# Splitting the weights of the layers' first halves in the DMA queue of a DeltaNet, S5 and pooling backbone

## The chip, the cores and the metric

The kernel runs on one core of a Trainium2 chip. The metric is the time of one execution on the device in microseconds; the time before is the median of three runs. The engines are named as in the profile: PE is TensorE's matmuls and PEld its weight loads, DVE is VectorE, ACT is ScalarE, POOL is GpSimd, and SP is the engine that only issues DMAs here. POOL can issue DMAs as well, on a queue of its own.

## What is computed

Two streams go through two layers with shared weights: 128 context tokens and 512 latent tokens, 1024 channels each, float32. The reference, cut to what matters:

```python
def trunk_layer(x, cond, s_dn, s_re, s_im, ...):
    mod = (silu(cond) @ w_ada + b_ada)[:, None, :]
    shift1, scale1, gate1, shift2, scale2, gate2 = split(mod, 6)
    h = rmsnorm(x, norm1_g) * (1 + scale1) + shift1
    q, k, v, z, dn_a, dn_b, u_ssm, u_pool, gates = split(h @ w_in, offsets)
    o_dn = deltanet_mixer(q, k, v, z, dn_a, dn_b, ...)   # 4 heads x 128, chunks, both directions
    o_ssm = s5_mixer(u_ssm, ...)                         # 32 groups, 64 complex states, both directions, GLU
    o_pool = pool_mixer(u_pool, ...)                     # centred windows 2, 4, 8, 16
    g_dn, g_ssm, g_pool = split(sigmoid(gates), 3)
    merged = g_dn * (o_dn @ w_branch_dn) + g_ssm * (o_ssm @ w_branch_ssm) + g_pool * (o_pool @ w_branch_pool)
    x = x + gate1 * (merged @ w_out)
    h = rmsnorm(x, norm2_g) * (1 + scale2) + shift2
    return x + gate2 * conv_ffn(h, ffn_w_up, ffn_conv, ffn_w_down)
```

A layer's first half is everything up to `x + gate1 * ...`, its second half is the ConvFFN.

## The kernel before

Activations lie with the channels on the partitions and all 640 tokens side by side, in two halves of 320 columns. A large product is made tile by tile: 128 output channels over 4 or 8 blocks of 128 input channels. This text calls one such tile with its weights a **piece**: a piece of 8 blocks has 512 KB of weights, a piece of 4 blocks 256 KB.

Products are made with float32r operands in three parts. Every operand is split into a high part, its cast to float32r, and a low part, the rest. `mm3` (L377) multiplies high by high, high by low and low by high (L384, L386, L388), so there are six matmuls of 320 columns per block, 48 in a piece of 8 blocks.

The weights come raw. `wraw` (L356) loads a piece on SP's queue into one of `WRAW` = 4 buffers. `wsplit` (L362) then splits it in steps of `WK` = 4 blocks: ScalarE casts 128x512 values into a `whi` tile, through a helper whose line in the profile is L235, and VectorE subtracts (L372):

```python
S.activation(hi, src, AF.Copy)
V.tensor_sub(lo, src, hi)
```

There are `WB` = 4 buffers of half a piece for each part. The tag `wraw` also holds the conditioning weights (`wada`, multiplied at L446).

In a first half two kinds of work run side by side. A **chain** is a long dependent computation: first the S5 scan, later DeltaNet. The S5 chain begins with products of its parameters on VectorE and POOL (L900, L901, L906). DeltaNet uses VectorE throughout (for example L1457, L1467) and POOL for scalings (L1534, L1535). **Side work** is a queue of pieces in `Weave` (L189), each with a cost, a function and, as a third entry, a function that fetches its weights. `Weave.run` pulls pieces as the chain yields costs, and `step` (L209) fetches the weights of the next piece just before it makes the current one. The pieces of a layer, in order: z gates and pooling inputs (`zgate`, `pool`, 4 each), the pooling branch's gates and projections in turn (`gated`, 8 pairs of 8 and 4 blocks), 8 of the q, k, v inputs (`qkv`), all beside the S5 scan; then the four GLU pieces (`glu`) and 8 pairs for the S5 branch, with no chain beside them, which this text calls the stage of the S5 gates; then 4 more of q, k, v and 8 gates beside DeltaNet. The projections of the DeltaNet branch, the output projection and the FFN take their weights through `Stream.tile` in plain loops.

The function texts set only the program's order; a scheduler then orders each engine's instructions. Each engine runs its own list strictly in that order, and a DMA waits in the list of the engine that issues it.

## Time and profile before

| | |
|---|---|
| median of three runs | 2593.4 us (2589.87 to 2594.01) |
| the profiled execution | 2591.93 us |
| its span in the profile | 2590.2 us, 43654 instructions |
| mean granted clock of TensorE | 0.973 |
| HBM read, written | 251.45 MB, 42.48 MB |

The profile shows one execution. Its span runs from the first instruction to the end of the last; the 1.7 us beside it are the rest of the execution's own time. Stages can be told from DMAs: in layer 0 the first GLU weight is asked for at 317.5 us (the end of the S5 chain), DeltaNet's first decay row at 534.9, the first weight of the output projection at 768.8, the first of the FFN at 810.9; in layer 1 the first half lies between about 1345 and 2070 us. Matmuls are pipelined: two of the same line that stand together in the timeline overlap, and the pace is the distance between starts, not the length of one.

### The profile page before, as it was taken

The numbers are of one execution on the slowest core, as the hardware profiler recorded it, in microseconds if no ns is written. First come the engines' busy times: TensorE is split into PE (matmuls) and PEld (weight loads), VectorE is DVE, ScalarE is ACT, GpSimd is POOL, SyncE is SP. The second block draws the span as 40 slices with busy tenths as digits, with TensorE's granted clock in tenths as the row PEclk, the third lists the DMA queues.
The fourth block names the chain that finished last, engine by engine and source line by source line (L and its number), as shares of the span: only waits on it lengthen the run. The fifth ranks groups of instructions, "written<-read, shape, count | busy, mean of one in ns | idle before, by whom it ended". The sixth has DMA issues, their size and how long they took to land. (4 is left out here: it accounts for less than half of the span.)

```text
span 2590.2 us, 43654 instructions
## 1 busy us (share of the span) xinstructions
PE 2440.7 (94%) x17225; PEld 2321.6 (90%) x17225; DVE 1608.3 (62%) x3250; ACT 989.8 (38%) x1792; POOL 555.2 (21%) x560
## 2 busy tenths in 40 slices
PE   7899989998889999999988999899989999999999
PEld 6688987997789988999988998799879899999998
DVE  5768863269866743553596687633897766445355
ACT  4242342363333531442443423424533354334243
POOL 3521320135342100000134404311445320000000
PEclk8899999999889999999999999999999999999999
DMA  9833327344253255322237232463454322222221
GB/s 309 162 112 94 91 64 233 114 127 140 94 178 95 74 172 178 98 67 81 75 115 103 59 113 79 118 197 99 138 166 160 112 66 74 74 74 78 78 66 66
DMA packets 382016, 297.29 MB, mean 115 GB/s; under 512 B 33706, under 2 KB 336500, under 8 KB 381812
## 3 DMA queue, kind: packets, MB, share of 16 engines
q1 hardware_dynamic: 377892, 286.53, 38.4%
q0 software_dynamic: 3552, 7.73, 1.2%
q8 instruction: 136, 2.23, 0.4%
q14 instruction: 68, 0.56, 0.1%
q10 hardware_dynamic: 368, 0.25, 0.0%
HBM read 251.45 MB, written 42.48 MB: 113 GB/s over the span
## 5 line engine op out<-in xcount | busy, mean ns | idle before, releaser
L384 PE MATMUL acc<-pg,whi 128*128 128x320 f32 x4064 | 943.2, 313 | 5.9 <-ACT pg L235 2.9
L388 PE MATMUL acc<-pg,wlo 128*128 128x320 f32 x4064 | 936.0, 311 | 8.0 <-DVE wlo L372 8.0
L386 PE MATMUL acc<-pg,whi 128*128 128x320 f32 x4064 | 938.0, 311 | 4.9 <-DVE pg L411 4.9
L372 DVE TENSOR_TENSOR wlo<-wraw,whi 128x512 fp32r<-128x512 f32 (+1 forms) x538 | 414.5, 776 | 524.3 <-ACT whi L235 518.1
L384 PEld LDWEIGHTS acc<-pg,whi 128*128 128x128 f32 x4064 | 681.4, 189 | 47.1 <-issue 16.7
L388 PEld LDWEIGHTS acc<-pg,wlo 128*128 128x128 f32 x4064 | 684.5, 189 | 10.5 <-DVE wlo L372 8.9
L386 PEld LDWEIGHTS acc<-pg,whi 128*128 128x128 f32 x4064 | 685.4, 189 | 6.0 <-DVE pg L411 5.4
L235 ACT ACTIVATE whi<-wraw 128x512 fp32r<-128x512 f32 (+1 forms) x538 | 331.7, 623 | 925.4 <-PE acc L386 723.0
L235 ACT ACTIVATE pg<-pg 128x640 f32<-128x640 f32 (+8 forms) x335 | 222.0, 682 | 262.5 <-DVE pg L1996 56.1
L235 ACT ACTIVATE pg<-sm 128x512 f32<-128x512 f32 (+9 forms) x245 | 109.5, 470 | 207.1 <-PE sm L1502 59.4
L235 ACT ACTIVATE pg<-acc 128x640 f32<-128x640 f32 (+3 forms) x196 | 127.0, 655 | 73.9 <-PE acc L388 49.5
L700 DVE SCALAR_TENSOR_TENSOR pg<-pg,cols_f 128x511 f32<-128x511 f32 (+1 forms) x130 | 65.9, 548 | 49.8 <-ACT pg L235 49.7
L411 DVE TENSOR_TENSOR pg<-pg,pg 128x640 fp32r<-128x640 f32 x84 | 68.6, 821 | 41.4 <-ACT pg L235 37.6
L713 POOL DMA_DIRECT2D pg<-in_ssm_lambda_re_dram x2 | 1.2, 583 | 407.9 <-ACT whi L235 407.9
L1685 POOL TENSOR_TENSOR pg<-pg,pg 128x640 f32<-128x640 f32 x21 | 38.9, 1855 | 226.1 <-DVE pg L1683 146.9
L691 DVE SCALAR_TENSOR_TENSOR pg<-acc,mod,pg 128x320 f32<-128x320 f32 x56 | 30.8, 549 | 78.3 <-PE acc L388 78.2
L235 ACT ACTIVATE pg<-acc,cols_f 128x640 f32<-128x640 f32 (+1 forms) x88 | 68.3, 776 | 0.0
L701 DVE SCALAR_TENSOR_TENSOR pg<-pg,cols_h 128x511 f32<-128x511 f32 (+1 forms) x130 | 65.6, 546 | 0.0
L446 PE MATMUL sm<-wada,silu_c 128*32 128x512 f32 x320 | 57.9, 627 | 8.0 <-DMA wada<-in_w_ada_dram 8.0
L1683 DVE SCALAR_TENSOR_TENSOR pg<-pg,acc 128x640 f32<-128x640 f32 x48 | 39.0, 817 | 40.9 <-PE acc L388 35.3
L906 POOL TENSOR_TENSOR pg<-pg,pg 128x512 f32<-128x512 f32 (+1 forms) x32 | 54.7, 1710 | 1.9
L901 POOL TENSOR_TENSOR pg<-s_cp,pg 128x640 f32<-128x640 f32 x16 | 27.6, 1725 | 127.4 <-PE acc L388 55.8
(392 smaller groups left out, 2960.8 us busy)
## 6 DMA issues: line engine op xcount, KB each, us to landing
wraw<-in_w_in_dram SPq DMA_DIRECT2D x96, 512.0 KB, 4.4
wraw<-in_ffn_w_up_dram SPq DMA_DIRECT2D x88, 512.0 KB, 3.9
wada<-in_w_ada_dram SPq DMA_DIRECT2D x80, 512.0 KB, 4.4
wraw<-in_ffn_w_down_dram SPq DMA_DIRECT2D x32, 512.0 KB, 3.9
mg_dram<-pg SPq DMA_DIRECT2D x32, 320.0 KB, 2.2
pg<-mg_dram SPq DMA_DIRECT2D x32, 320.0 KB, 5.2
wraw<-in_w_out_dram SPq DMA_DIRECT2D x16, 512.0 KB, 3.9
pg<-in_w_ada_dram SPq DMA_DIRECT2D x6, 1024.0 KB, 10.8
```

What stands on the lines that cost most here:

```text
L235: ins = self.engine.activation(out, in_, func, **kw)
L372: V.tensor_sub(lo, src, hi)
L384: PE.matmul(ps[:M, h, :HF], hi[:, k, :M], hh[:, h * HF:(h + 1) * HF], start=first and k == 0, stop=False)
L386: PE.matmul(ps[:M, h, :HF], hi[:, k, :M], hl[:, h * HF:(h + 1) * HF], start=False, stop=False)
L388: PE.matmul(ps[:M, h, :HF], lo[:, k, :M], hh[:, h * HF:(h + 1) * HF], start=False, stop=last and k == n - 1)
L411: V.tensor_sub(lo.r, src, hi.r)
L446: PE.matmul(ps[q:q + 32, :], silu_c[:, k, :], t[:, j * 512:(j + 1) * 512], start=k == 0, stop=k == KT - 1, tile_position=(0, q))
L700: V.scalar_tensor_tensor(y[:, b + 1:e], r[:, b:e - 1], w0, y[:, b + 1:e], op0=OP.mult, op1=OP.add)
L701: V.scalar_tensor_tensor(y[:, b:e - 1], r[:, b + 1:e], w2, y[:, b:e - 1], op0=OP.mult, op1=OP.add)
L906: E.tensor_tensor(oo, oo, t.f, op=OP.add if r else OP.subtract)
L1683: V.scalar_tensor_tensor(hv(g_.f), hv(g_.f), 1.0, ps[:, :, :HF], op0=OP.add, op1=OP.mult)
L1685: GP.tensor_tensor(g_.f, g_.f, mg.f, op=OP.add)
```

## The change

For 64 pieces of each layer (those with `dma=True`: all gates, z, pooling, q, k, v, GLU, and the projections of the pooling and S5 branches) the split is made another way. `wdma` has POOL issue a DMA that casts the weights to float32r while loading them into `whi`. ScalarE writes the negated high part into `wlo`, in one pass over the piece. POOL then issues a second DMA of the same weights that adds them onto `wlo`. VectorE and SP have no part in it. 44 of these pieces have 8 blocks, 20 have 4. `Weave` now fetches the weights of the next two pieces.

The constants change for all weights: a part of a piece is one tile of up to 8 blocks (`WK` = 8) with three buffers (`WB` = 3), so that `wsplit`, which stays for the other weights, makes one pass in place of two; there are three raw buffers; one page of the buffer arena is 128 columns smaller.

```diff
--- before.py
+++ after.py
@@ -35,10 +35,10 @@
 NSLOT = 82
 UNIT = 4
 PAGE = 2592 // UNIT
-PAGES = [5888] + [2592] * 2 + [2560] * 4 + [1280] * 11 + [2592]
+PAGES = [5760] + [2592] * 2 + [2560] * 4 + [1280] * 11 + [2592]
 EPS = 1e-6
-WRAW = 4
-WK, WB = 4, 4
+WRAW = 3
+WK, WB = 8, 3
 OFF_Q, OFF_K, OFF_V, OFF_Z, OFF_AB = 0, 512, 1024, 1536, 2048
 OFF_SSM, OFF_POOL, OFF_G = 2064, 2576, 3088
 POOL_WINDOWS = (2, 4, 8, 16)
@@ -194,7 +194,7 @@
         self.arena = arena
         self.q = deque()
         self.credit, self.scale = 0.0, 1.0
-        self.w = None
+        self.w = deque()
 
     def add(self, cost, fn, weights=None):
 
@@ -209,8 +209,12 @@
     def step(self):
         cost, fn, weights = self.q.popleft()
         self.arena.side = True
-        w = [self.w or weights()] if weights else []
-        self.w = self.q[0][2]() if self.q and self.q[0][2] else None
+        if weights and not self.w:
+            self.w.append(weights())
+        w = [self.w.popleft()] if weights else []
+        later = [x for _, _, x in self.q if x][:2]
+        while len(self.w) < len(later):
+            self.w.append(later[len(self.w)]())
         fn(*w)
         self.arena.side = False
         self.credit -= cost
@@ -374,6 +378,17 @@
             los.append(lo)
         return Blocks(his), Blocks(los)
 
+    def wdma(src, c0, nk):
+
+
+        v = src.rearrange("(k p) m -> p k m", p=P)[:, :, c0:c0 + P]
+        hi = wpool.tile([P, nk, P], F32R, name="whi", tag="whi", bufs=WB, padded_shape=[P, WK, P])
+        lo = wpool.tile([P, nk, P], F32R, name="wlo", tag="wlo", bufs=WB, padded_shape=[P, WK, P])
+        GP.dma_start(hi, v)
+        S.activation(lo, hi, AF.Copy, scale=-1.0)
+        GP.dma_start(lo, v, accum_op=OP.add)
+        return Blocks([hi]), Blocks([lo])
+
     def mm3(ps, w, hs, first=True, last=True, M=P):
 
         hi, lo = w
@@ -422,10 +437,12 @@
     class Stream:
 
 
-        def __init__(self, src, c0, ncols, nk=KT):
-            self.src, self.c0, self.nk = src, c0, nk
+        def __init__(self, src, c0, ncols, nk=KT, dma=False):
+            self.src, self.c0, self.nk, self.dma = src, c0, nk, dma
 
         def tile(self, m):
+            if self.dma:
+                return wdma(self.src, self.c0 + m * P, self.nk)
             return wsplit(wraw(self.src, self.c0 + m * P, self.nk, P), 0)
 
 
@@ -1663,7 +1680,7 @@
             return g_
 
         def gate_w(n, m):
-            return lambda: Stream(w_in, OFF_G + n * D, D).tile(m)
+            return lambda: Stream(w_in, OFF_G + n * D, D, dma=True).tile(m)
 
         def zgate(h, w):
 
@@ -1698,7 +1715,7 @@
                 if m == KT - 1:
                     free_pairs(ob)
 
-            return [(6.5, first, gate_w(n, m)), (3.3, second, lambda: Stream(wsrc, 0, D, 4).tile(m))]
+            return [(6.5, first, gate_w(n, m)), (3.3, second, lambda: Stream(wsrc, 0, D, 4, dma=True).tile(m))]
 
         pools = {}
 
@@ -1748,7 +1765,7 @@
 
 
         def tile_of(fn, m, src, c0, nk=KT):
-            return 0.82 * nk, lambda w: fn(m, w), lambda: Stream(src, c0, 0, nk).tile(m)
+            return 0.82 * nk, lambda w: fn(m, w), lambda: Stream(src, c0, 0, nk, dma=True).tile(m)
 
         def kq(m):
             return tile_of(qkv, m, w_in, 0)
```

The order of the engines' lists shows what moves, at three places.

VectorE's list at the start of the S5 chain in layer 0. L900 and L901 are the parameters' products, L906 their sums, L1674 the z gate's last step, L372 the subtraction. Before:

```order
L906 TENSOR_TENSOR pg18_13_132<-pg18_13_132,pg1_7_98 128x512
L1674 SCALAR_TENSOR_TENSOR pg7_29_1173<-pg7_29_1173,acc_1124 128x640
L906 TENSOR_TENSOR pg14_16_138<-pg14_16_138,pg5_11_126 128x512
L901 TENSOR_TENSOR pg18_13_132<-s5_bp_773,pg6_12_130 128x512
L906 TENSOR_TENSOR pg15_17_140<-pg15_17_140,pg5_11_126 128x512
L372 TENSOR_TENSOR wlo_1333<-wraw_1330,whi_1332 128x512
L372 TENSOR_TENSOR wlo_1337<-wraw_1330,whi_1336 128x512
L906 TENSOR_TENSOR pg17_19_176<-pg17_19_176,pg18_13_132 128x512
L2052 SCALAR_TENSOR_TENSOR pg13_15_136<-pg12_14_134,pg13_15_136 128x128
L372 TENSOR_TENSOR wlo_1494<-wraw_1491,whi_1493 128x512
```

With the change (L917, L918 and L923 are the same products and sums, L1691 the z gate, L2056 to L2069 the pooling sums, L945 a copy from PSUM):

```order
L923 TENSOR_TENSOR pg18_13_132<-pg18_13_132,pg1_7_98 128x512
L923 TENSOR_TENSOR pg14_16_138<-pg14_16_138,pg5_11_126 128x512
L923 TENSOR_TENSOR pg15_17_140<-pg15_17_140,pg5_11_126 128x512
L1691 SCALAR_TENSOR_TENSOR pg17_19_176<-pg17_19_176,acc_827 128x640
L917 TENSOR_TENSOR pg17_19_176<-s5_bp_761,pg6_12_130 128x512
L2056 COPY pg18_13_132<-pg13_15_136 128x512
L2061 TENSOR_TENSOR pg12_14_134<-pg18_13_132 128x513
L2066 TENSOR_TENSOR pg12_14_134<-pg12_14_134,cst_72 128x1
L2069 SCALAR_TENSOR_TENSOR pg13_15_136<-pg12_14_134,pg13_15_136 128x512
L945 COPY pg0_1_87<-sm_900 64x81x4
```

The three subtractions in between are gone, and the products and sums stand together.

POOL's list at the same place. Before, small loads and then the products:

```order
L317 DMA rows_h1_8060<-in_ffn_conv_dram 44x128
L731 MEMSET s5_dr_12133 128x128
L733 DMA s5_dr_12133<-in_ssm_d_dram 8x4x16
L901 ISA
L901 TENSOR_TENSOR pg0_1_87<-s5_cp_772,pg6_12_130 128x640
L2037 MEMSET pg18_13_132 128x1
L2038 MEMSET pg18_13_132 128x1
L2039 COPY pg18_13_132<-pg13_15_136 128x128
L900 TENSOR_TENSOR pg18_13_132<-s5_bp_773,pg6_12_130 128x512
```

With the change (L387 is the casting DMA, L389 the adding one):

```order
L387 DMA whi_822<-in_w_in_dram 128x8x128
L748 MEMSET s5_dr_11607 128x128
L750 DMA s5_dr_11607<-in_ssm_d_dram 8x4x16
L389 DMA wlo_813<-in_w_in_dram 128x8x128
L389 DMA wlo_818<-in_w_in_dram 128x8x128
L917 ISA
L917 TENSOR_TENSOR pg18_13_132<-s5_bp_761,pg6_12_130 128x512
L917 TENSOR_TENSOR pg14_16_138<-s5_bp_761,pg6_12_130 128x512
L917 TENSOR_TENSOR pg15_17_140<-s5_bp_761,pg6_12_130 128x512
L917 TENSOR_TENSOR pg11_28_1067<-s5_bp_761,pg6_12_130 128x512
L917 TENSOR_TENSOR pg12_14_134<-s5_bp_761,pg6_12_130 128x512
L389 DMA wlo_823<-in_w_in_dram 128x8x128
```

The high parts of the first three pieces (two more L387 stand just above these rows) are asked for ahead of the products, the low parts of two as well, and that of the third (wlo_823) after five products.

POOL's list in the stage of the S5 gates in layer 0. L1685 adds a projection to the sum of the branches. Before, nothing else stands there:

```order
L900 TENSOR_TENSOR pg1_7_98<-s5_cp_772,pg6_12_130 128x640
L906 TENSOR_TENSOR pg1_7_98<-pg1_7_98,pg5_34_3326 128x640
L1685 TENSOR_TENSOR pg1_7_98<-pg1_7_98,pg12_42_4110 128x640
L1685 TENSOR_TENSOR pg12_42_4110<-pg12_42_4110,pg18_43_4222 128x640
L1685 TENSOR_TENSOR pg17_44_4320<-pg17_44_4320,pg18_43_4222 128x640
```

With the change (L1702 is that addition; w_in is a gate's piece of 8 blocks, w_branch_ssm a projection's of 4):

```order
L387 DMA whi_4265<-in_w_branch_ssm_dram 128x4x128
L387 DMA whi_4299<-in_w_in_dram 128x8x128
L389 DMA wlo_4266<-in_w_branch_ssm_dram 128x4x128
L1702 TENSOR_TENSOR pg1_42_4112<-pg1_42_4112 128x640
L389 DMA wlo_4300<-in_w_in_dram 128x8x128
L387 DMA whi_4354<-in_w_branch_ssm_dram 128x4x128
L387 DMA whi_4388<-in_w_in_dram 128x8x128
L389 DMA wlo_4355<-in_w_branch_ssm_dram 128x4x128
L1702 TENSOR_TENSOR pg18_13_132<-pg18_13_132,pg12_14_134 128x640
L389 DMA wlo_4389<-in_w_in_dram 128x8x128
```

Two DMAs per piece now stand between the additions, and a piece's high part is asked for before the low part of the piece ahead of it.

## Rows read from the trace of the kernel before

**Rows 1.** The page, part 1: busy us (share of the span) and instructions of the engines, in one line.

```profile
PE 2440.7 (94%) x17225; PEld 2321.6 (90%) x17225; DVE 1608.3 (62%) x3250; ACT 989.8 (38%) x1792; POOL 555.2 (21%) x560
```

**Rows 2.** Windows: stretch and length; busy of PE, PEld, DVE, ACT, POOL; PEclk, DMA share, GB/s.

```profile
50.00:100.00 50.00, 46.49 (x305) 42.98 (x304) 31.28 (x111) 16.86 (x36) 12.85 (x21) 0.97 1.09 196
100.00:120.00 20.00, 8.58 (x28) 3.79 (x29) 19.96 (x16) 2.30 (x4) 19.37 (x16) 0.70 0.68 215
200.00:250.00 50.00, 43.59 (x291) 40.68 (x290) 44.27 (x140) 12.55 (x22) 11.44 (x21) 0.93 0.29 86
450.00:500.00 50.00, 50.00 (x343) 50.00 (x343) 12.06 (x17) 9.96 (x16) 9.67 (x6) 1.00 0.35 103
600.00:650.00 50.00, 39.80 (x257) 37.71 (x256) 47.42 (x82) 18.45 (x37) 25.07 (x22) 0.90 0.49 157
650.00:700.00 50.00, 41.93 (x343) 38.52 (x341) 44.95 (x90) 13.99 (x35) 14.21 (x10) 0.93 0.23 73
1850.00:1900.00 50.00, 42.30 (x294) 40.73 (x293) 47.96 (x93) 19.36 (x43) 27.03 (x24) 0.97 0.38 124
1900.00:1950.00 50.00, 43.67 (x351) 41.03 (x350) 47.63 (x102) 20.10 (x52) 16.71 (x13) 1.00 0.52 168
2150.00:2200.00 50.00, 50.00 (x343) 50.00 (x342) 28.72 (x50) 22.49 (x35) 0.00 (x0) 1.00 0.26 76
```

**Rows 3.** TensorE's waits, whole run: who waited for whom, us, times, longest.

```profile
PE sm L1463 <- DVE pg L1457: 9.6, 4, 6.4
PE acc L388 <- DVE wlo L372: 8.0, 1, 8.0
```

**Rows 4.** Timeline, VectorE and TensorE, 116 to 118 us: start, length, instruction, wait.

```profile
116.28 3.27 DVE L372 TENSOR_TENSOR wlo<-wraw,whi 128x512 fp32r<-128x512 f32 x2
...
117.91 0.90 PE L388 MATMUL acc<-pg,wlo 128*128 128x320 f32 x2 [8.04 <-DVE wlo L372]
```

**Rows 5.** Timeline, VectorE and TensorE, 612 to 627 us.

```profile
612.34 3.01 DVE L372 TENSOR_TENSOR wlo<-wraw,whi 128x512 fp32r<-128x512 f32 x1
...
626.21 0.68 DVE L372 TENSOR_TENSOR wlo<-wraw,whi 128x512 fp32r<-128x512 f32 x1
...
618.03 1.12 PE L1463 MATMUL sm<-cst,pg 128*128 128x128 f32 x4 [6.42 <-DVE pg L1457]
```

**Rows 6.** Lines of VectorE, 47 to 400 us, then 535 to 800 us.

```profile
L372 DVE TENSOR_TENSOR wlo<-wraw,whi 128x512 fp32r<-128x512 f32 x62 | 50.2, 816 | 36.5 <-ACT whi L235 35.6 <-PE acc L388 0.6
...
L372 DVE TENSOR_TENSOR wlo<-wraw,whi 128x512 fp32r<-128x512 f32 x31 | 37.8, 1222 | 15.7 <-ACT whi L235 10.7 <-PE acc L388 5.0
```

**Rows 7.** Timeline, TensorE, 454 to 456 us: two starts, one k apart.

```profile
454.22 0.45 PE L384 MATMUL acc<-pg,whi 128*128 128x320 f32 x2
...
455.10 0.46 PE L384 MATMUL acc<-pg,whi 128*128 128x320 f32 x2
```

**Rows 8.** DMA issues: count, KB each, median us from issue to landing.

```profile
wraw<-in_w_in_dram SPq DMA_DIRECT2D x96, 512.0 KB, 4.4
...
pg<-gr_dram POOLq DMA_DIRECT2D x20, 256.0 KB, 3.7
...
wraw<-in_w_branch_pool_dram SPq DMA_DIRECT2D x16, 256.0 KB, 2.8
...
pg<-in_ssm_b_re_dram POOLq DMA_DIRECT2D x2, 128.0 KB, 6.1
```

**Rows 9.** Lines of ScalarE by form: the cast of a whole raw weight.

```profile
L235 ACT ACTIVATE pg<-wraw 128x1024 fp32r<-128x1024 f32 x7 | 7.4, 1061 | 8.8 <-DMA wraw<-in_ffn_w_up_dram 7.2 <-DMA wraw<-in_w_in_dram 1.5
```

**Rows 10.** POOL's DMA issues (min/median/max ns; then by form, mean ns).

```profile
L1833 POOL DMA_DIRECT2D pg<-gr_dram x20: 538/579/627, 534.9 to 1897.8; - x20
...
L722 POOL DMA_DIRECT2D pg<-in_ssm_b_re_dram x2 | 2.3, 1126 | 12.1 <-ACT whi L235 12.1
```

**Rows 11.** Waits, whole run: ScalarE for a weight buffer, VectorE for POOL.

```profile
ACT whi L235 <- PE acc L386: 723.0, 351, 7.4
...
DVE pg L1555 <- POOL pg L1534: 18.2, 5, 5.7
```

## The prediction

> **What bounds the kernel now.** I read the busy line of the page first, then the windows, then the waits, then the timeline where a wait is long. TensorE is busy 2440.7 of 2590.2 us, VectorE 62%, POOL 21% [rows 1]. A mean over the run hides that the stages differ. In the second halves TensorE is never idle (50.00 of 50 from 2150 to 2200), and in the stage of the S5 gates it isn't either (450 to 500) [rows 2]. Nothing that frees another engine is worth anything there. What can be won lies in the first halves, where TensorE waits. From 100 to 120 us it is busy 8.58 of 20 us, at a granted clock of 0.70 (between its two levels of 1.2 and 2.4 GHz, after it had idled), while VectorE and POOL are both full (19.96 and 19.37). In the DeltaNet stages TensorE idles 10.2, 8.1, 7.7 and 6.3 us in four windows of 50, while VectorE is busy 45 to 48 [rows 2].
>
> The two longest waits of TensorE for VectorE say what VectorE was doing [rows 3]. The first, 8.04 us, ends at 117.91 with the subtraction that makes the low part of a weight: the subtraction stood in VectorE's queue behind the S5 products and ran at 116.28 [rows 4]. The second, 6.42 us, ends at 618.03 with a DeltaNet operation (L1457), and before it VectorE spent 3.01 us on one such subtraction that takes 0.68 us at 626 [rows 5]. The 3.01 falls where POOL runs its own products. The Trainium skill (SBUF — State Buffer, Who interferes with whom) says that a VectorE instruction with two SBUF inputs and a POOL instruction that reads SBUF hold each other up; these rows agree.
>
> **What is removed.** In each layer 44 pieces have 8 blocks of rows and 20 have 4, so 44 x 2 + 20 = 108 subtractions of 128x512 leave VectorE, 216 in both. Their price is not one number: 0.816 us each before 400 us (62 of them, 50.2 us), 1.222 each from 535 to 800 (31) [rows 6]. ScalarE keeps one pass per piece, 1.061 us for 1024 columns [rows 9], in place of two shorter ones: nothing, as it is free over half of the time in every window of rows 2. The loads on SP are gone; each was hidden and counts nothing.
>
> *Start of S5, layer 0.* Three pieces are asked for ahead of the products in POOL's queue, so TensorE has side work where it waited 8.04 us. The 8.58 us of work at clock 0.70 would take 6.0 at full clock, 2.6 less. The two make 10.6; the third low part stands behind five POOL products, so I take **-9** (bounds 0 and -11.4, the idle of that window).
>
> *DeltaNet stages.* 12 pieces per layer run beside them: 24 x 1.222 = 29 us less of VectorE's time where it is nearly full. TensorE can't win more than it idles: 18.3 us in the two windows of layer 0, 14.0 in those of layer 1. Not all of its idling is VectorE's; I take a bit over half, **-18** (bounds 0 and -32).
>
> *Rest of S5.* From 200 to 250 us TensorE idles 6.4 with VectorE at 44.27 [rows 2]. Half of that in each layer: **-6** (bounds 0 and -13).
>
> **What is added.** 256 DMAs are issued by POOL. The trace has no cast, no adding DMA, and none of 512 KB on this queue, so I bound them. A 512 KB weight on SP's queue lands 4.4 us after its issue, a 256 KB one 2.8; 256 KB on POOL's queue take 3.7, so 0.9 more; the slowest on that queue, 2048 short runs, take 6.1 [rows 8]. For the high part I take 4.4 + 0.9 = 5.3 (bounds 4.4 and 6.1). The adding DMA moves the same bytes from HBM and reads its target as well. Bounds: 4.4, and 2 x 5.3 = 10.6. I take 5.3, the row of a like transfer, and leave the second read to a rival.
>
> *The buffer loop in the S5 gates.* There TensorE has nothing but pieces, 8 pairs of 8 and 4 blocks per layer. Six matmuls of one block take 0.88 us [rows 7], so a piece lasts 7.0 or 3.5, a pair 10.6. With three buffers the high part of piece i+3 can be asked for only when piece i is done, and it is needed two pieces later, after 10.6 us. The way is high part 5.3, ScalarE 1.06 [rows 9], low part 5.3: 11.7, so 1.1 late. What is late in one round is a lead in the next, so it costs half: 0.55 x 16 pairs = **+9**. With 4.4 for both transfers the way is 9.9, and nothing is lost. With 10.6 it is 17.0, and 3.2 x 16 = 51 are lost.
>
> *Start of layer 0.* The DMA engines are full from 50 to 100 us (share 1.09, 196 GB/s) [rows 2]. The three first pieces are now read twice: 1.5 MB more, 8 us at that rate. TensorE has the conditioning products meanwhile: **+4** (bounds 0 and +8).
>
> *POOL's queue.* An issue takes 0.58 us (128 runs) to 1.13 (2048 runs) [rows 10], some 0.8 for these 1024 runs, so 256 x 0.8 = 205 us more on an engine that is busy 555 of 2590. VectorE waited 18.2 us, five times, for POOL's DeltaNet products [rows 11]. One issue more in front of each is 5 x 0.8: **+4** (bounds 0 and +18). The waits for a free buffer and for ScalarE's pass now also stand in this queue; what they would cost is rival D.
>
> *Second halves.* Whole pieces of 1024 columns, three buffers, in place of halves with four: TensorE is full there, and ScalarE and VectorE are used 22 and 29 of 50 [rows 2], so 0. If that cover went, the first piece of each change of weights would be one half pass later, about 0.6.
>
> **Sum.** -9 - 18 - 6 + 9 + 4 + 4 = -16 on the profiled execution's 2591.9 gives 2575.9. The median of the runs is 1.5 above that execution, so I forecast **2577**.
>
> **Rivals.** *A, the forecast:* 2577. If nothing is lost in the loop, -33 + 8 = -25 gives 2568; the full bounds of the gains, -56, with the costs as taken, +17, give 2554; three quarters of the gains, -25 + 17, give 2585. Its own range is 2554 to 2585.
>
> *B, the loop of three buffers becomes the bound (slower).* The adding DMA has a second read. By rows 8, 256 KB more cost 4.4 - 2.8 = 1.6 us, so 512 KB read again cost 3.2, and it lands after 8.5. The way is 5.3 + 1.06 + 8.5 = 14.9, 4.3 late, 2.15 x 16 = 34 lost in the gate stage: -33 + 34 + 8 = +9, or 2602. With 10.6 it is +26, 2619; if the 8 pairs of the pooling branch in each layer pay a third of that too (17), 2636. It decides from the point where 16 x half the lateness eats the other terms' 25: 3.1 us late, that is an adding DMA of 7.3 us. For it: with the queue's own rows near 6 us for short runs there are 1.2 us to spare. Against it: nothing on this queue takes 7.3 in rows 8, and the second read is on chip. The Trainium skill (Collectives: The Full Stack, The bandwidth ceiling) says that the add in the DMA engines is no cost but its two source reads halve the rate; by it this rival's 2602 would be the time. No run here shows it.
>
> *C, the relief doesn't reach TensorE.* The chains of S5 and DeltaNet run through ScalarE, POOL and TensorE too. If half of the gain comes, 16.5, it meets 17 of costs: 2594, no change. For it: TensorE's two longest waits on VectorE sum to only 17.6 us [rows 3].
>
> *D, POOL's queue holds the chains up.* The high part's DMA waits on POOL until TensorE is done with a buffer. ScalarE waited for that 723.0 us in 351 times, 2.06 each [rows 11], and could afford it. On POOL such a wait stands ahead of S5 and DeltaNet products: 44 pieces a layer there, 88 x 2.06 = 181 us. POOL is busy up to half of the time in these windows [rows 2], so about half of that is hidden, and of the other 90 TensorE covers part with side work. With half of them: -33 + 17 + 45 = +29, 2622; with all, 2667. The Trainium skill (SBUF — State Buffer, SBUF: two separate sides) adds that descriptors written by POOL stall behind VectorE operations that use both ports. Against that: 20 issues in the DeltaNet stages stay between 538 and 627 ns, beside a VectorE that is nearly full [rows 10].
>
> That the change doesn't do what it says is excluded: in the order of the new program the high part of a piece stands ahead of the low part of the one before, so pieces do run ahead.
>
> **How the numbers follow.** A 0.46, B 0.28, C 0.13, D 0.13. A measurement of this kernel tells changes over 0.2% (5 us) from none, so faster is A, 0.46; same is C, 0.13; slower is B and D, 0.41. The range 2548 to 2640 leaves out the far end of A, the far end of D and little else.
>
> **What would show it.** Right: no wait of TensorE near 117 us, DeltaNet windows with TensorE above 44 of 50, the gate stage still near 50, the adding DMA landing under 7 us. B would show as waits of TensorE on the adding DMA in the gate stage and landing times above 7.3. D would show as POOL idle ahead of S5 or DeltaNet products with a weight DMA in front. C would show VectorE lighter, with TensorE's idle time as before but ended by ScalarE or POOL. The forecast is wrong if the gate stage grows by over 10 us a layer.

## The result, and the profile after

The median is 2775.98 us (2773.29 to 2780.28, four runs) against 2593.7 for the kernel before in the same comparison: 1.0708 times as long, 95% interval 1.0689 to 1.0726. The forecast was 2577, and 2776 lies above the whole range.

The busy line of the page after, which answers to [rows 1]:

```profile
PE 2500.3 (90%) x17225; PEld 2362.7 (85%) x17225; DVE 1458.5 (53%) x2881; ACT 952.5 (34%) x1551; POOL 818.2 (30%) x816
```

VectorE got 150 us lighter, as meant, and POOL 263 us heavier. TensorE does the same 17225 matmuls but is busy 60 us longer, and the span grew by 183, so 123 us of the growth are idle time and 60 the same matmuls taking longer (mean granted clock 0.947, before 0.973). The windows, in the form of [rows 2]; stages lie later here, so the windows from 2050 and from 2350 stand beside those from 1850 and from 2150 before:

```profile
100.00:120.00 20.00, 17.09 (x97) 13.50 (x96) 17.56 (x12) 2.35 (x3) 17.26 (x18) 0.83 0.95 222
200.00:250.00 50.00, 41.33 (x252) 37.42 (x252) 42.03 (x146) 12.39 (x22) 24.19 (x33) 0.83 0.65 113
450.00:500.00 50.00, 39.18 (x245) 34.65 (x244) 2.92 (x7) 6.02 (x8) 17.96 (x15) 0.90 0.90 170
650.00:700.00 50.00, 38.45 (x253) 37.20 (x253) 47.18 (x61) 12.13 (x22) 31.01 (x29) 0.84 0.66 131
1450.00:1500.00 50.00, 38.48 (x245) 37.68 (x244) 12.85 (x14) 10.77 (x18) 17.93 (x21) 0.90 1.10 134
2050.00:2100.00 50.00, 34.09 (x206) 30.18 (x204) 44.87 (x94) 14.97 (x33) 20.19 (x17) 0.86 0.49 130
2350.00:2400.00 50.00, 50.00 (x343) 50.00 (x342) 28.74 (x43) 21.56 (x29) 0.00 (x0) 1.00 0.26 74
```

From 100 to 120 us TensorE is busy 17.09 us in place of 8.58, and the wait of 8.04 us in [rows 3, 4] is gone. But in the stage of the S5 gates (450 to 500), where it was never idle, it now idles 10.8 of 50 us with VectorE at 2.92, and the DMA engines are at 0.90 where they were at 0.35. From 1450 to 1500, at the start of layer 1's S5 stage, they stand at 1.10 and move 134 GB/s; in the kernel before the like stretch, 1380 to 1430, has 0.87 at 114 GB/s. The second half of layer 1 is full as before.

The waits of the whole run (us, times, longest):

```profile
POOL wlo L389 <- ACT wlo L239: 308.6, 89, 14.1
...
ACT wlo L239 <- DMA whi<-in_w_in_dram: 270.6, 68, 12.3
...
POOL whi L387 <- PE acc L403: 153.6, 50, 13.1
...
PE acc L403 <- DMA wlo<-in_w_in_dram: 80.3, 24, 8.2
```

Each row says who waited for whom. The last is the one on TensorE's own path: 24 times it waits for an adding DMA of a piece of 8 blocks, up to 8.2 us. The queues (packets, MB, share of 16 engines' span) and the landings:

```profile
q0 software_dynamic: 228832, 120.99, 30.0%
q1 hardware_dynamic: 265252, 229.90, 27.7%
...
whi<-in_w_in_dram POOLq DMA_DIRECT2D x88, 512.0 KB, 6.2
wlo<-in_w_in_dram POOLq DMA_DIRECT2D x88, 512.0 KB, 6.8
```

The 512 KB of a casting DMA land after 6.2 us and those of an adding one after 6.8; a plain load took 4.4 [rows 8]. These times run from the start of the issue, so POOL's own time for the issue is inside them (in the rows of e18 one is issued at 453.34, lands after 13.3, and TensorE goes on at 466.66). POOL's queue holds the 16 engines 30.0% of the span for 228832 packets, 58 ns each (0.300 x 16 x 2772.9 us, divided by the count); SP's 265252 take 46 ns. POOL's own time for the issues (us, mean ns, idle time before them):

```profile
L389 POOL DMA_DIRECT2D wlo<-in_w_in_dram x88 | 140.6, 1598 | 258.2 <-ACT wlo L239 212.8 <-ACT dn_tok L239 22.8 <-ACT s_hall L239 6.4
L387 POOL DMA_DIRECT2D whi<-in_w_in_dram x88 | 96.8, 1100 | 87.9 <-PE acc L403 84.1 <-PE acc L401 3.5 <-issue 0.4
```

All 256 issues take 328 us, where the prediction counted 205.

Where the time went is read from landmarks on TensorE: the last start of the last S5 product (L999 before, L1016 after), the first DeltaNet input (L1289 after), the last transposition of DeltaNet (L1893 after), in each layer. The S5 stage of layer 0 ends by them at 376.8 in the kernel before; the 317.5 given above as the end of the chain is only when the first GLU weight is asked for. Two of the rows behind them, before and after (ns; first and last start in us; forms); the last start, 1662.0 and 1790.4, ends the S5 stage of layer 1:

```profile
L999 PE MATMUL sm<-pg,pg x128: 270/273/472, 295.2 to 1662.0; 128*81 128x128 f32 x128
```

```profile
L1016 PE MATMUL sm<-pg,pg x128: 272/273/421, 301.2 to 1790.4; 128*81 128x128 f32 x128
```

The table gives, for this kernel and all the experiments, what each stage of the profiled execution took longer than in the kernel before (us). "Between" runs from DeltaNet of layer 0 to the end of S5 in layer 1, so it holds the second half of layer 0. Where the text says how much a run loses beside the chains over e1, it takes the sum of the columns S5, DeltaNet (both) and "between", and subtracts that of e1.

| run | S5, 0 | gates, 0 | DeltaNet, 0 | between | gates, 1 | DeltaNet, 1 | rest | span |
|---|---|---|---|---|---|---|---|---|
| the change | 22.8 | 29.5 | 8.2 | 67.9 | 16.6 | 37.5 | 0.2 | 182.7 |
| e1 constants | -5.8 | -1.3 | -2.6 | 24.0 | -3.7 | 23.3 | 1.2 | 35.1 |
| e2 gate stage | -6.2 | 27.7 | -6.4 | 26.9 | 20.3 | 23.9 | -1.2 | 85.0 |
| e3 chains | 16.2 | -1.1 | 8.0 | 67.2 | -3.0 | 39.5 | 0.2 | 127.0 |
| e4 no add | -19.5 | 5.7 | -9.0 | 9.2 | 0.8 | 22.8 | 1.0 | 11.0 |
| e5 add 1 block | -12.1 | 4.9 | -11.1 | 38.5 | 0.2 | 20.1 | -2.0 | 38.5 |
| e6 second cast | 6.0 | 15.7 | -1.4 | 36.4 | 5.8 | 29.4 | -1.4 | 90.5 |
| e7 halves | 25.8 | -2.4 | 9.5 | 51.7 | 0.8 | 41.7 | 0.9 | 128.0 |
| e8 raw 3 | -5.4 | 3.2 | -2.3 | 6.0 | 7.1 | -0.7 | -1.2 | 6.7 |
| e9 relief | -21.0 | -1.0 | -1.7 | -9.3 | 7.1 | 2.0 | -2.3 | -26.2 |
| e10 one ahead | 8.1 | 1.4 | -9.2 | 23.9 | -4.2 | 28.4 | 0.9 | 49.3 |
| e11 one issue | -0.6 | 38.5 | 2.1 | 16.8 | 18.2 | 37.3 | 0.8 | 113.1 |
| e12 POOL time | 5.0 | -3.4 | -6.5 | 45.1 | -3.0 | 20.8 | 1.0 | 59.0 |
| e13 four buffers | 26.1 | 8.2 | 12.8 | 110.2 | 19.5 | 52.3 | 0.0 | 229.1 |
| e14 four, plain | 29.7 | 4.0 | 3.2 | 65.2 | 16.9 | 27.0 | -0.4 | 145.6 |
| e15 POOL sub | -1.5 | -5.3 | -3.3 | -2.3 | 6.6 | 1.1 | 0.2 | -4.5 |
| e16 copy on ScalarE | 4.4 | -2.2 | -2.0 | 3.1 | 3.3 | -0.2 | -0.7 | 5.7 |
| e17 pass on VectorE | -6.7 | 32.6 | -7.7 | 24.1 | 28.8 | 29.0 | -1.6 | 98.5 |
| e18 no conditioning | -7.0 | 9.0 | -8.0 | 26.0 | 6.3 | 22.8 | 0.5 | 49.6 |

One execution stands behind each row, and stages move by some 7 us for no reason that an edit gives (gates, 1 in e8, e9 and e15), so only larger numbers are used.

### The profile page after: what moved, and what is told of

Read it like the earlier page. It is cut to its first block, busy times and chain, and to the rows that moved or that the text cites. A ratio compares the mean times of both kernels' runs of the same rounds, so it can differ in the third digit from the quotient of the medians.

```text
span 2772.9 us, 43018 instructions
## 1 busy us (share of the span) xinstructions
PE 2500.3 (90%) x17225; PEld 2362.7 (85%) x17225; DVE 1458.5 (53%) x2881; ACT 952.5 (34%) x1551; POOL 818.2 (30%) x816
## 2 busy tenths in 40 slices
DMA packets 494651, 353.88 MB, mean 128 GB/s; under 512 B 35754, under 2 KB 449140, under 8 KB 494452
## 3 DMA queue, kind: packets, MB, share of 16 engines
q0 software_dynamic: 228832, 120.99, 30.0%
q1 hardware_dynamic: 265252, 229.90, 27.7%
## 4 chain that ended last, share of the span: by engine, by line
PE 49%; DVE 10%; DMA 8%; issue 5%; POOL 3%; ACT 2%; SPq 0%; POOLq 0%; DVEq 0%; ACTq 0%
PE acc L403 13%; PE acc L399 13%; PE acc L401 13%; DMA wlo<-in_w_in_dram 2%; DMA whi<-in_w_in_dram 2%; ACT pg L239 1%; DMA wraw<-in_ffn_w_down_dram 1%; DMA wraw<-in_ffn_w_up_dram 1%; PE sm L536 1%; DVE wlo L376 1%; DVE pg L1444 1%; DVE pg L598 1%; DVE pg L1404 1%; PE acc L420 1%; PE sm L1431 1%
## 5 line engine op out<-in xcount | busy, mean ns | idle before, releaser
L403 PE MATMUL acc<-pg,wlo 128*128 128x320 f32 x4064 | 953.6, 316 | 84.9 <-DMA wlo<-in_w_in_dram 80.3
L399 PE MATMUL acc<-pg,whi 128*128 128x320 f32 x4064 | 958.9, 318 | 36.5 <-ACT pg L239 25.8
L401 PE MATMUL acc<-pg,whi 128*128 128x320 f32 x4064 | 952.0, 315 | 2.8 <-DVE pg L426 2.8
L399 PEld LDWEIGHTS acc<-pg,whi 128*128 128x128 f32 x4064 | 695.2, 193 | 75.3 <-ACT pg L239 40.9
L401 PEld LDWEIGHTS acc<-pg,whi 128*128 128x128 f32 x4064 | 698.6, 193 | 5.4 <-DVE pg L426 4.0
L376 DVE TENSOR_TENSOR wlo<-wraw,whi 128x1024 fp32r<-128x1024 f32 (+2 forms) x169 | 214.3, 1271 | 282.3 <-ACT whi L239 282.0
L239 ACT ACTIVATE whi<-wraw 128x1024 fp32r<-128x1024 f32 (+2 forms) x169 | 168.3, 997 | 422.1 <-PE acc L401 317.5
L239 ACT ACTIVATE wlo<-whi 128x1024 fp32r<-128x1024 f32 (+1 forms) x128 | 118.3, 925 | 441.0 <-DMA whi<-in_w_in_dram 270.6
L389 POOL DMA_DIRECT2D wlo<-in_w_in_dram x88 | 140.6, 1598 | 258.2 <-ACT wlo L239 212.8
L387 POOL DMA_DIRECT2D whi<-in_w_in_dram x88 | 96.8, 1100 | 87.9 <-PE acc L403 84.1
L586 POOL TENSOR_SCALAR pg<-pg,ada_a 128x320 f32<-128x320 f32 (+2 forms) x27 | 26.7, 996 | 126.1 <-DVE pg L708 59.5
L717 DVE SCALAR_TENSOR_TENSOR pg<-pg,cols_f 128x511 f32<-128x511 f32 x98 | 49.5, 548 | 20.6 <-ACT pg L239 18.5
```

The lines of the kernel that those rows point to most:

```text
L239: ins = self.engine.activation(out, in_, func, **kw)
L387: GP.dma_start(hi, v)
L389: GP.dma_start(lo, v, accum_op=OP.add)
L399: PE.matmul(ps[:M, h, :HF], hi[:, k, :M], hh[:, h * HF:(h + 1) * HF], start=first and k == 0, stop=False)
L401: PE.matmul(ps[:M, h, :HF], hi[:, k, :M], hl[:, h * HF:(h + 1) * HF], start=False, stop=False)
L403: PE.matmul(ps[:M, h, :HF], lo[:, k, :M], hh[:, h * HF:(h + 1) * HF], start=False, stop=last and k == n - 1)
```

## The experiments

Three theories are named W, Q and K in the expectations: the way of a piece over its two transfers is too long (W), the DMAs in POOL's list hold up the chains (Q), the new constants cost by themselves (K). Medians below are of 4 runs (e4 8, e15 and e16 10), beside 2590 to 2596 for the kernel before in the same comparisons.

### The parts of the change

**e1, the constants alone.** The two other `dma=True` go in the same way.

```diff
-            return 0.82 * nk, lambda w: fn(m, w), lambda: Stream(src, c0, 0, nk, dma=True).tile(m)
+            return 0.82 * nk, lambda w: fn(m, w), lambda: Stream(src, c0, 0, nk, dma=False).tile(m)
```

> All pieces take the plain load and the subtraction again; what is left of the change are the buffers (three of 8 blocks, three raw) and the fetch two pieces ahead. Theory W (the way of a piece over two POOL transfers is longer than the pieces it runs ahead of) and theory Q (the DMAs in POOL's list hold up the chains) both expect the loss gone: 2575 to 2600 us. Theory K (three buffers and three raw ones cost by themselves: the second half of layer 0 grew by 14 us and the turn into layer 1 by 26) expects about 2594 + 40 = 2634.

Measured 2621.1 (ratio 1.0123, 1.0097 to 1.0149). So 155 of the 182 us belong to the DMAs (2776.0 - 2621.1), net of what the relief brings; W and Q missed the other part, of which K had foreseen the kind.

**e2, the gate stage alone by DMA, and e3, all but the gate stage** (the conditions below for e2, their opposite for e3).

```diff
-            return lambda: Stream(w_in, OFF_G + n * D, D, dma=True).tile(m)
+            return lambda: Stream(w_in, OFF_G + n * D, D, dma=(n == 1)).tile(m)
...
-            return 0.82 * nk, lambda w: fn(m, w), lambda: Stream(src, c0, 0, nk, dma=True).tile(m)
+            return 0.82 * nk, lambda w: fn(m, w), lambda: Stream(src, c0, 0, nk, dma=(nk == 4)).tile(m)
```

> Only the GLU pieces and the 8 pairs of the S5 branch, the stage with no chain beside it, are split by DMA. That stage grew by 29 us in layer 0 and 17 in layer 1. W expects these 46 us on top of the run with the constants alone, and waits of TensorE on the adding DMA there. Q expects next to nothing on top (under 10), since no chain stands behind POOL's list in that stage.

> The opposite of the run before: the pieces that run beside the S5 scan and DeltaNet are split by DMA, the stage of the S5 gates is not. W in the gate stage alone: 2776 - 46 = 2730. If the losses of the stages add up, the losses over the kernel before of this run and of the run with the gate stage alone sum to 182; if the two interact (one stage's lateness hidden in the next), the sum is off by over 20.

Measured 2674.2 (1.0329, 1.0311 to 1.0348) and 2710.1 (1.0474, 1.0447 to 1.0500). Over e1 these are 53 and 89, and e1 itself lost 30; 30 + 53 + 89 = 172 of 182, so the losses add up. (82.6 + 118.5 = 201 over the kernel before holds the constants twice.) Q alone can't explain the 53.

**e4, no adding DMA.**

```diff
-        GP.dma_start(lo, v, accum_op=OP.add)
```

> The changed kernel without the adding DMA: the low part stays the negated high part, so the products of the low parts are left out of the computation in value, while every other instruction stays. W: the way is the casting DMA's 6.2 us and ScalarE's 1.1, under the 10.6 us of a pair, so TensorE's waits on the low part go and the gate stage returns: 2640 or less. Q with the waits of the casting DMA for free buffers (153.6 us on POOL) as the cause: at most half of the loss goes, 2690 or more.

Measured 2603.9 (1.0055, 1.0037 to 1.0073): 172 us hang on the adding DMA, and casting DMA and relief together gain 17 over e1. POOL waits longer for free buffers than in the change (153.6) and it costs nothing that can be seen:

```profile
POOL whi L387 <- PE acc L402: 227.0, 47, 11.4
```

The DMA's landing and issue show that the casting DMA, too, is quicker without the adding one (5.3 and 0.915 us, in the change 6.2 and 1.100):

```profile
whi<-in_w_in_dram POOLq DMA_DIRECT2D x88, 512.0 KB, 5.3
```

```profile
L387 POOL DMA_DIRECT2D whi<-in_w_in_dram x88 | 80.5, 915 | 218.7 <-PE acc L402 97.4 <-issue 59.1 <-ACT wlo L239 26.0
```

**e5, the add on one block.**

```diff
-        GP.dma_start(lo, v, accum_op=OP.add)
+        GP.dma_start(lo[:, :1], v[:, :1], accum_op=OP.add)
```

> The adding DMA stays for every piece, at its place in POOL's list and behind ScalarE's pass, but carries only the first of the 8 (or 4) blocks; the low parts of the other blocks are left out of the computation in value. Without the adding DMA the time was 2604, with it 2776, so 172 us hang on it. W (its transfer is too long): 2610 to 2640. Q (its wait for ScalarE, 308 us, blocks POOL's list, however little it carries): 2700 or more.

Measured 2632.1 (1.0161, 1.0146 to 1.0177), in W's range. POOL still waits 280.6 us for ScalarE's pass, as in the change (308.6). That wait, 128 more issues (POOL is busy 741.2 us in place of 636.2) and a short transfer together cost 28 over e4.

**e6, a second cast in place of the add.**

```diff
-        GP.dma_start(lo, v, accum_op=OP.add)
+        GP.dma_start(lo, v)
```

> The second DMA writes the same bytes to the same place with the same waits, but casts instead of adding (the low parts are the high parts, so the low products are left out in value). If the add itself (reading its target) is the price: its landing falls from 6.8 toward the casting DMA's 6.2 or below and its issue from 1.60 to 1.10 us on POOL, and the time falls below 2720. If the price is a second transfer of 512 KB in the way, adding or not: within 25 of 2776.

Measured 2679.2 (1.0339, 1.0317 to 1.0361). Same bytes, the same places in POOL's list, 97 us less: over half of the DMAs' price is the add itself, its longer issue and its later landing together. Landings and issues of the two transfers:

```profile
whi<-in_w_in_dram POOLq DMA_DIRECT2D x88, 512.0 KB, 5.5
wlo<-in_w_in_dram POOLq DMA_DIRECT2D x88, 512.0 KB, 4.9
```

```profile
L387 POOL DMA_DIRECT2D whi<-in_w_in_dram x88 | 79.8, 907 | 110.4 <-PE acc L403 98.3 <-PE acc L401 12.0
L389 POOL DMA_DIRECT2D wlo<-in_w_in_dram x88 | 79.7, 906 | 243.4 <-ACT wlo L239 204.7 <-ACT dn_tok L239 22.1 <-ACT s_hall L239 7.6
```

4.9 us against the add's 6.8, 0.91 us of POOL against 1.60.

**e12, POOL's time alone.** Five memsets of 128x32 follow e5's short add.

```diff
+        for _ in range(5):
+            GP.memset(idle, 0.0)
```

> The run with an adding DMA of one block (2632) plus five small memsets on POOL per piece, some 0.8 us, about what the issues of the changed kernel take longer than in that run (0.82 us per piece of 8 blocks); the low parts are left out as there. If POOL's time in front of the chains' products is the price (Q): 2660 or more, a good part of the 144 us between 2632 and 2776. If the way of the transfers is (W): 2632 to 2645.

Measured 2651.0 (1.0212, 1.0186 to 1.0238), between the two: the memsets take 92.7 us of POOL, 0.72 per piece, and cost 19. POOL is now busy 818.0 us, as in the change (818.2), and the time is still 125 us below it. POOL's time is a real price, but not the main one.

### The way of a piece

**e7, half pieces in six buffers.**

```diff
-WK, WB = 8, 3
+WK, WB = 4, 6
...
+        for k in range(0, nk, WK):
+            n = min(WK, nk - k)
...
+            GP.dma_start(hi, v[:, k:k + n])
+            S.activation(lo, hi, AF.Copy, scale=-1.0)
+            GP.dma_start(lo, v[:, k:k + n], accum_op=OP.add)
```

> The same bytes in half pieces: tiles of 4 blocks, six buffers of each part, so a buffer comes free after 3.5 us of products instead of 7.0 and the way of a half is 5.1 + 0.6 + 4.9 and its issues. W: five halves are 17.5 us of products against a way of 12, so the 46 to 53 us of the gate stage go and part of the rest: 2720 or less. Q: POOL issues 2 x (0.9 + 1.3) = 4.4 us per piece of 8 blocks in place of 2.7 and has twice the waits in its list: 2776 or more.

Measured 2720.9 (1.0503, 1.0483 to 1.0523): 55 less, at W's border. The gate stage is back (-2.4 and 0.8), though POOL issues 216 pairs of DMAs in place of 128, and TensorE's waits for the adding DMA are gone, from 80.3 us in 24 times to one:

```profile
PE acc L408 <- DMA wlo<-in_w_in_dram: 2.7, 1, 2.7
```

Beside the chains the run still loses 90 over e1, the change 97. What is lost there is not these waits. POOL is busier here, 959.4 us, so the run doesn't say what it is.

**e13, four whole buffers, and e14, its control.**

```diff
-WRAW = 3
-WK, WB = 8, 3
+WRAW = 2
+WK, WB = 8, 4
-PAGES = [5760] + [2592] * 2 + [2560] * 4 + [1280] * 11 + [2592]
+PAGES = [5760] + [2592] * 2 + [2560] * 4 + [1280] * 11 + [1536]
-        later = [x for _, _, x in self.q if x][:2]
+        later = [x for _, _, x in self.q if x][:3]
```

> The changed kernel with four buffers of 8 blocks for each part and the fetch three pieces ahead; the room comes from a raw buffer (two are left) and a smaller last page of the arena. Issues, bytes and transfers stay. W says that a piece takes (way + products) / buffers, so a pair of pieces in the gate stage takes 2 x (15.7 + 5.3) / 4 = 10.5 us, its product time, in place of 14: the 46 us of the gate stage go, and most of the waits on the adding DMA beside the S5 scan (38 us); the time is 2776 - 70 = 2706 or less, even with two raw buffers. If it is the transfers' load or POOL's time: 2760 or more.

> The control for the run before: the same four buffers, two raw buffers, page and fetch three ahead, with every piece on the plain load and the subtraction. Three raw buffers alone cost 10 us, so two should cost more: 2620 to 2670 if the raw buffers decide; 2600 or less if it was the three buffers of 8 blocks that cost the 30 us of the run with the constants alone.

Measured 2827.4 (1.0910, 1.0880 to 1.0939) and 2745.9 (1.0597, 1.0564 to 1.0631). The absolute forecast missed, because the room taken costs 154 by itself. DMAs in place of plain loads cost 81.5 here, with three buffers 155. In the gate stage it is 4.2 and 2.6 over the control, with three buffers 30.8 and 20.3 over e1; in the S5 stage of layer 0 it is -3.6, with three buffers 28.6. But the control is a poor one: its plain loads have two raw buffers, and it is itself some 20 us longer than e1 in the gate stage of layer 1 and some 35 in the S5 stage of layer 0. Set beside the change itself, e13 shortens only the gate stage of layer 0 (29.5 to 8.2); that of layer 1 (16.6 and 19.5) and the S5 stage (22.8 and 26.1) stay. So the pair supports W in one stage and settles nothing in the others. Beside DeltaNet and between, 80 us remain over the control, with three buffers 69 over e1.

**e11, one issue per piece.**

```diff
-        GP.dma_start(hi, v)
+        S.activation(hi, wraw(src, c0, nk, P), AF.Copy)
```

> The changed kernel with the high part made as before (plain load on SP into one of three raw buffers, cast by ScalarE) and only the low part by the adding DMA: one issue per piece on POOL in place of two, no wait for a free buffer in POOL's list, the same bytes. The load can run ahead in the raw buffers, so the way from a free buffer is 2 x 1.06 + 1.6 + 6.8 = 10.5 us in place of 15.7. W: the gate stage returns and the time is 2700 or less. If the adding transfers themselves (their load on the DMA engines) are the price wherever they stand: 2740 or more.

Measured 2694.2 (1.0395, 1.0367 to 1.0423). The time fits W, its reason doesn't: the gate stage grew by 38.5. The raw loads came late themselves, in ScalarE's timeline:

```profile
453.42 1.06 ACT L239 ACTIVATE whi<-wraw 128x1024 fp32r<-128x1024 f32 x1 [6.87 <-DMA wraw<-in_w_in_dram]
```

Beside the chains, however, this run loses only 17 over e1, against 97 in the change and a gain of 35 without the add (e4). Yet it moves the same bytes, 353.88 MB, and every adding DMA is in place, issued as long (1.59 us) and landing no sooner:

```profile
q1 hardware_dynamic: 377892, 286.53, 36.2%
q0 software_dynamic: 116192, 64.36, 18.5%
...
wlo<-in_w_in_dram POOLq DMA_DIRECT2D x88, 512.0 KB, 7.4
```

So neither the bytes nor the add alone make the loss beside the chains; it takes both DMAs of a piece on POOL.

**e17, the pass on VectorE, gate stage only.** An idea that failed.

```diff
-        S.activation(lo, hi, AF.Copy, scale=-1.0)
+        V.tensor_scalar(lo, hi, -1.0, None, op0=OP.mult)
```

> The run with the gate stage alone by DMA (2674; with no piece by DMA 2621), with the pass that writes the negated high part on VectorE in place of ScalarE, in that stage only. In ScalarE's list this pass stands behind the gate's tanh, which waits for the product of the piece now on TensorE; the traces show it at 420.10 for a high part asked for at 407.34. VectorE's list has one step per pair that waits for a product. If the place in ScalarE's list is half of the lateness: 2650 or less, and the stage grows by under 14 us a layer in place of 28 and 20. If only the two transfers and the pass themselves count, or VectorE's list is as bad: 2665 to 2680.

Measured 2694.6 (1.0382, 1.0364 to 1.0401), no better than e2. The place in ScalarE's list is not the cause: on VectorE the pass waits, in most pieces, for the high part itself:

```profile
DVE wlo L388 <- DMA whi<-in_w_branch_ssm_dram: 103.6, 13, 9.0
...
DVE wlo L388 <- DMA whi<-in_w_in_dram: 69.3, 15, 12.2
```

**e18, e2 without the conditioning loads of that stage.**

```diff
-                nc.sync.dma_start(t, a["w_ada"][l, k * P:(k + 1) * P, c0:c0 + 1024])
+                if grp != 2:
...
+                    t_ = cst[:, :512] if grp == 2 else t[:, j * 512:(j + 1) * 512]
```

> The run with the gate stage alone by DMA (2674; with no piece by DMA 2621), and the conditioning products of that stage read a constant tile in place of their weights (left out in value): the products stay, the loads of 512 KB on SP's queue that run beside the pieces, 13 or 14 a layer, go, and so do their raw buffers. Single transfers of POOL's queue landed after 12 to 14 us there while four or five others were under way. If these bursts make the rest of the lateness, the stage grows by under 14 us a layer in place of 28 and 20, and the time is 2650 or less. If the three buffers alone make it: 2665 to 2680.

Measured 2642.5 (1.0194, 1.0177 to 1.0212): the stage's growth fell from 27.7 and 20.3 to 9.0 and 6.3. With plain loads the conditioning loads cost nothing there: in e1 TensorE is busy 126.4 of the 126.4 us of layer 0's stage. What the run removes is seen in the trace of the change, POOL's timeline in that stage:

```profile
433.73 1.45 POOL L387 DMA_DIRECT2D whi<-in_w_in_dram  x1
448.20 0.77 POOL L387 DMA_DIRECT2D whi<-in_w_branch_ssm_dram  x1 [13.03 <-PE acc L403]
452.46 0.88 POOL L387 DMA_DIRECT2D whi<-in_w_in_dram  x1 [3.50 <-PE acc L403]
453.34 1.61 POOL L389 DMA_DIRECT2D wlo<-in_w_in_dram  x1
```

ScalarE's and TensorE's:

```profile
448.82 1.05 ACT L239 ACTIVATE wlo<-whi 128x1024 fp32r<-128x1024 f32 x1
```

```profile
466.66 0.90 PE L403 MATMUL acc<-pg,wlo 128*128 128x320 f32 x2 [7.29 <-DMA wlo<-in_w_in_dram]
467.36 0.74 PE L399 MATMUL acc<-pg,whi 128*128 128x320 f32 x2
...
470.56 0.70 PE L399 MATMUL acc<-pg,whi 128*128 128x320 f32 x2
471.09 0.46 PE L401 MATMUL acc<-pg,whi 128*128 128x320 f32 x2
471.39 0.46 PE L403 MATMUL acc<-pg,wlo 128*128 128x320 f32 x2
```

The landings of the two DMAs of that piece, issued at 433.73 and 453.34:

```profile
whi<-in_w_in_dram POOLq DMA_DIRECT2D x1, 512.0 KB, 14.3
```

```profile
wlo<-in_w_in_dram POOLq DMA_DIRECT2D x1, 512.0 KB, 13.3
```

And the DMA engines from 448 to 467 us (busy tenths in 40 slices) with SP's loads in that time:

```profile
DMA  0002999960000879999999999999999999999999
...
wada<-in_w_ada_dram SPq DMA_DIRECT2D x4, 512.0 KB, 6.1
```

The high part landed after 14.3 us, at 448.0, and ScalarE's pass follows at 448.82, behind an instruction that had waited for TensorE. The low part was asked for at 453.34, behind the DMA that had waited 3.50 us for a buffer, and landed after 13.3: TensorE waits 7.29 us for it. Four conditioning weights were under way then, and the DMA engines were full from 455 on. Without the conditioning loads no adding DMA took over 9.2 us (e2, then e18; all shapes):

```profile
DMA to landing us min/median/max: 4.2/6.5/16.0
```

```profile
DMA to landing us min/median/max: 4.3/5.5/9.2
```

The medians moved much less: the 512 KB adding DMAs of the stage land after 7.0 us in both layers of e2, and after 6.5 and 6.6 in e18.

After the wait TensorE's pairs start 0.53 us apart until 471.09 and 0.29 after it. The granted clock is 0.50 from 467.4 to 471 and 1.00 from 471.5 to 474, its two levels of 1.2 and 2.4 GHz: the 4.43 us of work at half speed add 2 us to a wait of 7.

### The relief, and whether it can be had

**e8, three raw buffers.**

```diff
-WRAW = 4
+WRAW = 3
```

> The kernel before with three raw buffers in place of four and nothing else. The run with the constants alone lost 30 us over the kernel before. If the raw buffers are the cause (the second half of layer 0 lost 7 us of TensorE's time from 900 to 1100, where the conditioning weights share these buffers): 2594 + 10 to 30. If it is the parts of 8 blocks or the fetch two ahead: 2594.

Measured 2600.7 (1.0043, 1.0026 to 1.0060), 10 slower. In the first 280 us of layer 0's second half, where the conditioning weights share these buffers, TensorE lost 6 (kernel before, then e8):

```profile
835.00:1115.00 280.00, 277.90 (x1873) 258.44 (x1872) 143.49 (x280) 108.39 (x184) 12.19 (x14) 1.00 0.42 125
```

```profile
830.40:1110.40 280.00, 271.87 (x1820) 250.63 (x1819) 140.97 (x275) 104.94 (x180) 12.17 (x14) 1.00 0.40 124
```

**e9, the relief alone**, on the kernel before; `dma` marks the same 128 pieces.

```diff
-            V.tensor_sub(lo, src, hi)
+            if dma:
+                S.activation(lo, hi, AF.Copy, scale=-1.0)
+            else:
+                V.tensor_sub(lo, src, hi)
```

> The kernel before, its buffers and its loads untouched, but ScalarE writes the low part of the same 128 pieces as the negated high part: 216 subtractions leave VectorE and nothing is added to POOL or the DMA queues (the low parts of these weights are left out of the computation in value). It prices the relief alone. If the prediction's gains of 33 us are real: 2560 or less. If the relief doesn't reach TensorE (its rival C): 2585 to 2600.

Measured 2569.5 (0.9908, 0.9891 to 0.9926), between the two: 22 us, two thirds of the 33. They lie in the S5 stages (-21.0, -9.3), nothing that can be told beside DeltaNet (-1.7, 2.0). The run is not quite the relief alone: ScalarE makes 216 more passes (busy 1109.9 us, before 989.8).

**e10, the constants with the fetch one ahead.**

```diff
-        later = [x for _, _, x in self.q if x][:2]
+        later = [x for _, _, x in list(self.q)[:1] if x]
```

> The run with the constants alone (2621), with the fetch one piece ahead as before. If the fetch two ahead costs by putting ScalarE's casts in front of the chains' work: 2600 or less. If the parts of 8 blocks and the three raw buffers cost it (10 us for the raw buffers are measured): 2610 to 2630.

Measured 2636.1 (1.0163, 1.0138 to 1.0188), 15 slower than e1 and above both ranges: the fetch two ahead helps, so the larger parts in fewer buffers, raw ones among them, cost the more.

**e15, half of the subtractions beside the S5 scan on POOL, and e16, 32 copies of the scan on ScalarE**, both on the kernel before (first and second pair of lines).

```diff
-            V.tensor_sub(lo, src, hi)
+            (GP if pool and k else V).tensor_sub(lo, src, hi)
...
-                V.tensor_copy(X[:SP, 1:1 + NK, r, gs], vv[:SP])
+                S.activation(X[:SP, 1:1 + NK, r, gs], vv[:SP], AF.Copy)
```

> The kernel before with the relief made another way: of the pieces of 8 blocks beside the S5 scan POOL makes the second half's subtraction, 48 in both layers, and VectorE the first. The relief of all 216 was worth 22 us, nearly all of it beside the S5 scan. POOL's products of this size take 1.4 us, 48 x 1.4 = 67 us more on POOL. If half of the relief comes: 2580. If POOL's chain products behind the subtractions are as late as VectorE's were: 2590 or more.

> The kernel before with 32 copies of the S5 chain (64 x 324, 485 ns on VectorE) moved to ScalarE, which is used under half beside the scan. It takes 16 us off VectorE in the stage where the relief was worth something, with no DMA and nothing on POOL. If VectorE's time there is what counts: 2580 to 2588. If ScalarE's copies stand in the way of the other copies of the same chain: 2594 or more.

Measured 2589.0 (0.9987, 0.9973 to 1.0002), no difference that can be told, and 2598.0 (1.0024, 1.0011 to 1.0038), a little slower. No version that computes the whole beats the kernel before.

## Why the prediction was wrong

The runs, one step at a time, give the sum that should have stood there: constants +27 (e1, against 2593.7), relief and casting DMA -17 (e4), a short adding DMA with its waits and issues +28 (e5), a second transfer of full size +47 (e6), adding in place of casting +97 (the change): 182. Rivals B and D were set as alternatives; both came, on top of a cost of the constants that stood nowhere.

*Gains, -33.* Right in kind, measured at -22 on the old buffers. The step on DeltaNet (-18) failed: a stage in which VectorE is full 45 of 50 us and TensorE idles need not be bound by VectorE's queue; relief there moved nothing that can be told (e9). The rest of S5 (-6) was too small. The start of S5 (-9) came in time, but nothing ties it to the relief, so that was luck: the wait near 117 is gone, and the chain's first transposition (L918 before, L935 after) starts at 115.1 in place of 123.0. In e9, with the relief, it starts at 116.9; but in e1 and e8, where all subtractions stay, at 114.6 and 117.7. Two of the signs set for being right failed: the gate stage, and DeltaNet windows with TensorE above 44 (38.45 from 650 to 700). The sign set for being wrong, a gate stage longer by over 10 us a layer, came (29.5 and 16.6).

*The buffer loop, +9.* In the gate stage it cost 46 in the change, 53 in e2 against e1. Rival B had its mechanism, and its sign (TensorE waiting for the adding DMA in that stage) came. But the test that I put between A and B, a landing of 7.3 us, was the wrong one: the median was 6.8, under it. Even the measured medians don't give the loss: in the prediction's own rule 6.2 + 1.06 + 6.8 = 14.1 is 3.5 late, 28 us by this estimate. Left out were the wait of one piece's low part behind another's high part in POOL's list (3.50 us in the rows of e18) and above all the spread of the landings. I took the medians of [rows 8] into a stage in which 13 conditioning loads of 512 KB a layer fall beside doubled weight traffic. Without those loads two thirds of the loss go, with medians of the adding DMA only 0.5 us lower and a longest landing of 9.2 in place of 16.0 (e18); with half pieces in six buffers all of it (e7). And I counted the loop only where TensorE has nothing but pieces; 28.2 of the 80.3 us of its waits for adding DMAs fall beside the S5 scan of layer 1. The Trainium skill (Collectives: The Full Stack, The bandwidth ceiling) has an add halve the rate by its second source read; by it, with the prediction's price of a second read, the landing would have been 8.5, an estimate. The trace lies between: 6.8 against 4.9 for the cast.

*POOL's queue, +4.* Beside the chains, where I counted this and 4 for the start, the DMAs cost 89 (e3 against e1), relief already taken off: the term that was furthest off. An issue was taken as 0.8 us from shapes of 128 and 2048 runs; they take 1.10 and 1.60. Some 0.7 us more per piece cost 19 (e12), and the short add with its wait for the pass and its issues 28 (e5). Rival D's 45 is near the sum of these two, but not for its reason: it priced the high part's wait for a free buffer, and e4, where that wait is longer (227.0 us), loses nothing by it. The waits named, and the issue time beside them, were the place to look; the size was luck.

*Second halves, 0.* Layer 1's stayed as it was ("rest" grew by 0.2), but in layer 0's first 280 us three raw buffers in place of four cost 6 (e8); the conditioning weights use these buffers too. I gave the constants no term of their own. At 27 they alone turn the forecast of -16 into a loss.

*What stays open.* Beside the chains the change loses 97 over e1, and the runs rule out three single causes: the casting DMA without the add costs nothing, with the relief it gains 35 (e4), the adding DMA alone with the same bytes costs 17 (e11), and without TensorE's waits for the adding DMA 90 still remain (e7). It takes both DMAs of a piece on POOL. How much of that is their issues and waits in POOL's list, ahead of the chains' products, and how much their transfers on one queue, no run separates. Nor is it settled why DeltaNet of layer 1 lost 20 or more in every run with the new buffers; three raw buffers alone don't do it (e8, -0.7), nor does the fetch two ahead (e10 has one ahead and loses 28.4). And why the smaller page and two raw buffers of e14 cost so much is not known.
